# A recurrent time-mixing kernel on one core: three clearings move, and the last tile's store and logarithm are split differently

## The chip, the cores and the metric

One core of one Trainium2 chip. The metric is the device time of one execution in microseconds; lower is better. A core has five engines with a queue of instructions each: TensorE (PE in the profile; its weight loads are PEld), VectorE (DVE), ScalarE (ACT), GpSimd (POOL) and SyncE (SP). They run side by side and wait for one another through semaphores. DMAs are issued from SP, ACT or POOL and carried out by 16 DMA engines.

## What is computed

`w`, `u` have 256 channels; `k`, `v` and the output are 16 x 2048 x 256 in float32. For each batch and channel a recurrence runs over 2048 steps:

```python
ww = u + kk
qq = np.maximum(pp, ww)
e1 = np.exp(pp - qq); e2 = np.exp(ww - qq)
output[b, t, :] = (e1 * aa + e2 * vv) / (e1 * bb + e2 + 1e-08)
ww = pp - w + kk
qq = np.maximum(ww, kk)
e1 = np.exp(ww - qq); e2 = np.exp(kk - qq)
aa = e1 * aa + e2 * vv
bb = e1 * bb + e2
pp = qq
```

## The kernel before, in words

**Tiles.** 2048 steps are 16 stages (`NST`) of 128 steps. A stage has four tiles, each of four batches, so there are 64 tiles `n` (`NP`). A tile of `k` or `v` is 128 partitions x 4 x 256, 512 KB. Each stage's 128 steps are two halves of 64; within a half the recurrence is written as matrix products, and a small state passes from half to half.

**Per tile.** PE writes the rows of decay and bonus into PSUM (`rows`, L201: 64x64 pieces from `CO` and from the rows' tile `WU`, made of `w` and `u`) and adds the sums of `k` (`logs`, L207). ACT takes the exponential into `EZR` (L210). DVE or POOL casts `v` to bfloat16 (`cast_v`, L214), and DVE multiplies (`times_v`, L219). PE sums per half into `TOT` (`sums`, L245). Ten tiles later PE forms denominator and numerator (`apply`, L322, with the matrices `Id`, `IdN`, `S`, `SN`), ACT inverts the denominator as Exp(-Ln(x)) (L330 and L338, 128x1024 each), DVE multiplies (L350) and the result is stored in three pieces: 256 KB by SP (L363) and two of 128 KB (`piece`, L356), both by SP, or one by SP and one by POOL for the last tiles (`shared`). The very last tile, 63, is inverted and multiplied in two halves (`parts`).

**Per stage** a chain of small instructions turns the sums into the next state: `copy_sums`, `turn`, `state_logs` (ACT, L262), `state_frames` and on (DVE, on the small tiles `U`, `G`, `TB`), `state_spread` into `CB`, then four PE matmuls (`turn_back`, L302, with `Id`). Some elements of `U`, `G`, `TB` and `CB` are never written by that chain and must be cleared once beforehand.

**What sets the order.** Every part is a *step* with a due time (`place`). A loop at the end of the function takes, again and again, the step with the earliest due time whose predecessors are done and whose buffer is free, and writes its instructions into the engines' queues. The queues are in order. Every engine writes before this loop what stands ahead of it in the function: the start.

**The start, in the order of each queue.** DVE: clears `WUf`, the 128x256 tile that will hold `w` and `u` in a few of its rows (L124), then `M1`, `I1`, `Z`, `COf`, `Sel`, `low`; builds `NLE`, `NLZ`, `CO`, `OH` with POOL's selects and iotas between; clears the state's tiles (L231 to L236, nine memsets); then, as the first step of the loop (due time -9.17, `mats`), scales four matrices (L182); then the first rounding of `k` (`round_k`, L194), the rows' tile (`make_rows`, L175 and L176), the second rounding. POOL: the load of `u` into `WUf`, selects, iotas, selects, the loads of tiles 3 and on. ACT: the load of `w` into `WUf`, then the table of functions. SP: three loads of `k` and three of `v`. PE: 26 matmuls on zeros (`Z`, L149), which only keep it running, then 12 more and the first rows.

**The end.** The last tile's exponentials, products and stores, then a line of the launcher (L480): each engine drains, SP waits for every DMA, and the engines meet in a handshake.

Of the kernel before, what the change touches and what calls it, by code (L numbers as in the profile page):

```python
# [7 lines left out]
F32 = mybir.dt.float32  # L8
# [3 lines left out]
ACT = mybir.ActivationFunctionType  # L12
# [3 lines left out]
def kernel(  # L16
# [9 lines left out]
    K = tc.keep_in_program_order  # L26
    PE, DVE, SC, POOL, SP = nc.tensor, nc.vector, nc.scalar, nc.gpsimd, nc.sync
# [5 lines left out]
    D = 2 * Dm  # L33
    NP = 4 * NST
# [10 lines left out]
    RS = 2.0 ** -20  # L45
    CAP = 54.0
    BIG = 1e30
# [24 lines left out]
    rpool = ctx.enter_context(tc.tile_pool(name="rpool", bufs=NRD))  # L72
# [14 lines left out]
    def matrix(name, dt):  # L87
        return consts.tile([128, 128], dt, tag=name, name=name)
# [10 lines left out]
    def how(n):  # L99
        return "D" if n < BYSP else FIRST[n] if n < len(FIRST) else PLAN[n % len(PLAN)]  # L100
# [4 lines left out]
    def load_k(n):  # L105
        if how(n) != "C":
            KR[n] = raw(opool, "ot") if n < BYSP else raw(kppool, "kf")
            K((SP if n < BYSP else POOL).dma_start(out=KR[n], in_=rows_of(k, n)))  # L108
        else:
            KR[n] = kpool.tile([128, 4, Dm], F32R, tag="kr", name="kr")  # L110
            K(POOL.dma_start(out=KR[n], in_=rows_of(k, n)))
# [6 lines left out]
    WUf = rpool.tile([128, 2, D], F32, tag="rd", name="WUf")[:, 0, 0:Dm]  # L118
# [2 lines left out]
    def row_wu(queue, x, g):  # L121
        K(queue.dma_start(out=WUf[g::32, :], in_=bass.AP(tensor=x.tensor, offset=x.offset, ap=[[0, 4], list(x.ap[0])])))

    K(DVE.memset(WUf, 0.0))  # L124
    load_k(0)
    row_wu(POOL, u, 1)
    row_wu(SC, w, 0)
# [50 lines left out]
    mats = {name: matrix(name, BF16) for name in ("Id", "IdN", "S", "SN")}  # L178
# [11 lines left out]
    X = [psx.tile([128, 2, D], F32, tag=f"X{a}", name=f"X{a}") for a in range(2)]  # L190
# [31 lines left out]
    AS, D1, L1, A0, FR, BC, A2 = range(7)  # L222
    U_of = [consts.tile([128, 7, 32, 3], F32, tag=f"U{j}", name=f"U{j}") for j in range(2)]
    G_of = [consts.tile([128, 3, 32, 3], F32, tag=f"G{j}", name=f"G{j}") for j in range(2)]
    TB_of = [consts.tile([128, 2, 32, 3], F32, tag=f"TB{j}", name=f"TB{j}") for j in range(2)]
    CB_of = [consts.tile([128, 4, 128], BF16, tag=f"CB{j}", name=f"CB{j}") for j in range(2)]
    AB = consts.tile([128, 2, 32, 3], F32, tag="AB", name="AB")
    st = {}

    for j in range(2):  # L230
        K(DVE.memset(CB_of[j].bitcast(F32), 0.0))  # L231
        K(DVE.memset(U_of[j][:, FR, :, 0:1], -BIG))
        K(DVE.memset(G_of[j][:, :, :, 0:1], 0.0))
    K(DVE.memset(U_of[0][:, D1, :, 0:1], -100.0))
    K(DVE.memset(U_of[0][:, L1, :, 0:1], 0.0))
    K(DVE.memset(TB_of[0][:, :, :, 0:1], 0.0))  # L236

    def sums(n):
        c, p = divmod(n, 4)
# [70 lines left out]
    RD, NUM, OT = {}, {}, {}  # L310
# [14 lines left out]
    def den(n, a):  # L325
        apply(X[a], n, ("S", "Id"), 1)

    def log_den(n, a):
        rd = rpool.tile([128, 2, D], F32, tag="rd", name="rd")
        K(SC.activation(rd, X[a], ACT.Ln, scale=RS))  # L330
        RD[n] = rd

    def parts(n):
        return (slice(0, 1), slice(1, 2)) if n == NP - 1 else (slice(0, 2),)

    def inverse(n):
        for i in parts(n):
            K(SC.activation(RD[n][:, i], RD[n][:, i], ACT.Exp, scale=-1.0))  # L338

    def by_x(n):  # L340
        return n >= NP - XT and n % 2 == 1
# [11 lines left out]
    def piece(n, h, queue):  # L353
        c, p = divmod(n, 4)
        t0 = c * TC + HS * (1 - h)
        K(queue.dma_start(out=out[4 * p + 2:4 * p + 4, t0:t0 + HS, :].rearrange("n t d -> t n d"), in_=OT[n][HS * h:HS * h + HS, 2:4, :]))  # L356

    def shared(n):
        return n >= BYPOOL or BYQ[n % len(BYQ)] == "P" and n >= BYF
# [5 lines left out]
            piece(n, h, SP)  # L365

    def store_rest(n):
        piece(n, 1, POOL)


    ops, free = {}, {"K": NK, "KP": NKP, "V": NV, "N": 1, "RD": NRD, "OT": NOT, "VB": NVB}
# [1 line left out]
    def step(name, place, fn, args=(), after=(), take=None, give=(), mode=0):  # L373
        key = name if isinstance(name, str) else " ".join(map(str, name))
        ops[name] = dict(place=AT.get(key, place), fn=fn, args=args, after=list(after), take=take, give=give, mode=mode)

    for n in range(NP):
        c, j = divmod(n, 4)
        early = n < BYSP
        vb = "OT" if n < VOT else "V"  # L380
        put = lambda key: n + P[key][j]
        lead = SOON * max(0.0, 1 - n / UNTIL)
        lag = LAG - sum(n < x for x in LAGS)
        m = n + lag - lead
        tail = n >= NP - LAG
        place = lambda key: m + (P["TAIL"][key] + (n - NP + LAG) * P["TAIL"]["step"] if tail else P["OUT"][key][int(n + lag + 2) % 4])
        kb = "OT" if early else "KP" if how(n) != "C" else "K"
        if n:
            step(("LK", n), n + P["LK"], load_k, (n,), [("LK", n - 1)], kb)
        else:  # L390
            free["OT"] -= 1
        step(("LV", n), n + P["LV"], load_v, (n,), [("LV", n - 1)] + ([("LK", n)] if n else []), vb)
        if how(n) != "C":
            step(("RK", n), put("RK"), round_k, (n,), [("LK", n), ("RK", n - 1)], "K", [kb])
        for q in range(2):
            step(("R", q, n), n + P["R"][q], rows, (n, q), ["wu", ("R", 1 - q, n - 1 + q)], "X", mode=3)
            step(("L", q, n), n + P["L"][q], logs, (n, q), [("R", q, n), ("LK", n), ("RK", n), ("L", 1 - q, n - 1 + q)], None,
                 ["K"] if q else [], 1)
            step(("X", q, n), n + P["X"][q], exps, (n, q), [("L", q, n), ("NUM", n - RING), ("S", n - RING)], None, ["X"])
        step(("CV", n), put("CV"), cast_v, (n,), [("LV", n), ("CV", n - 1)], "VB", [vb])  # L400
        step(("TV", n), put("TV"), times_v, (n,), [("X", 1, n), ("CV", n), ("TV", n - 1)], None, ["VB"])
        step(("S", n), put("S"), sums, (n,), [("TV", n), ("S", n - 1)] + ([("CS", c - 1)] if j == 0 else []), mode=2)
        if j == 3:
            s = P["STATE"][0 if c == 0 else 2 if c == NST - 1 else 1]
            for i, (name, fn, *after) in enumerate((
                    ("CS", copy_sums, ("S", n)), ("TU", turn, ("CS", c), ("CH", c - 1)), ("SL", state_logs, ("TU", c)),
                    ("FR", state_frames, ("SL", c), ("SN", c - 1)), ("OF", state_offsets, ("FR", c)),
                    ("SW", state_weights, ("OF", c)), ("CH", state_chain, ("SW", c), ("KP", c - 1)),
                    ("SS", state_spread, ("CH", c)), ("TK", turn_back, ("SS", c), "mats"), ("BK", copy_back, ("TK", c)),
                    ("SN", state_next, ("OF", c)), ("KP", state_keep, ("CH", c)))):  # L410
                if not (name in ("SN", "KP") and c + 1 == NST):
                    step((name, c), n + s[i] - lead * SHARE, fn, (c,), after, mode=1)
        step(("DEN", n), place("DEN"), den, (n,), [("BK", c), ("DEN", n - 1), "mats"], "X", mode=3)
        step(("LN", n), place("LN"), log_den, (n,), [("DEN", n), ("INV", n - 1)], "RD", ["X"])
        step(("INV", n), place("INV"), inverse, (n,), [("LN", n)])
        step(("NUM", n), place("NUM"), num, (n,), [("BK", c), ("TV", n), ("NUM", n - 1), "mats"], "X" if by_x(n) else "N", mode=3)
        step(("MUL", n), place("MUL"), mult, (n,), [("NUM", n), ("INV", n), ("MUL", n - 1)], "OT", ["X" if by_x(n) else "N", "RD"])
        step(("ST", n), place("ST"), store, (n,), [("MUL", n), ("ST", n - 1)], None, [] if shared(n) else ["OT"])
        if shared(n):
            step(("SQ", n), place("SQ"), store_rest, (n,), [("ST", n)], None, ["OT"])  # L420
    step("mats", P["mats"], make_matrices)
    step("wu", P["wu"], make_rows)

    quiet = False
# [60 lines left out]
```

## Time and profile before

| | us |
|---|---|
| runs of the kernel before | 290.93, 292.04, 292.12 (median 292.04) |
| profiled execution, whole | 291.05 |
| its span, first to last instruction | 289.3 |

| engine | busy us | share of the span | instructions |
|---|---|---|---|
| PE | 272.0 | 94% | 3263 |
| PEld | 139.5 | 48% | 3263 |
| DVE | 246.1 | 85% | 423 |
| ACT | 258.1 | 89% | 290 |
| POOL | 176.9 | 61% | 219 |

The DMAs moved 101.21 MB at a mean of 350 GB/s; in the first 30 us, when there are only loads, 348 to 350 GB/s from 8 us on.

How to read it: a line of the profile names engine, source line, operation, output<-input and shape. Times are from the span's start. "Idle before" is the time for which the engine stood still ahead of an instruction, and what ended that. The granted clock of TensorE was 0.988 of full speed over the span. A `q` behind an engine's name (SPq, POOLq) marks its sequencer: DMA issues, semaphores, drains.

### The profile page before, as it was taken

To read this page: it belongs to the slowest core of one execution; us is meant where nothing else is said; L and a number is where in the kernel's file an instruction comes from. 1 tells how busy PE (TensorE), PEld (TensorE's weight loads), DVE (VectorE), ACT (ScalarE), POOL (GpSimd) and SP (SyncE) were. 2 spreads that over 40 slices of the span, in tenths; PEclk is the share of its full clock that TensorE was granted. 3 is DMA by queue.
4 is the path that set the end of the run, shared out by engine and by line. 5 is a ranking of instruction groups with operands and counts; after the bars stand their busy time and mean duration, and the time that the engine had idled before them with its cause. 6 is when DMAs were issued, how large, how long until landed. Compare 5 with 4: busy or idle time off the path is not lost.

```text
span 289.3 us, 8057 instructions
## 1 busy us (share of the span) xinstructions
PE 272.0 (94%) x3263; PEld 139.5 (48%) x3263; DVE 246.1 (85%) x423; ACT 258.1 (89%) x290; POOL 176.9 (61%) x219
## 2 busy tenths in 40 slices
PE   7899999999999999999999999999999999997750
PEld 6445744444545455444545454554545455444330
DVE  6666889989898989899897979899898989797860
ACT  1587399999999999999999999999999999997890
POOL 7267367675767686675757686775757674422230
PEclk9999999999999999999999999999999999999995
DMA  7999999999999999999999999999999999896895
GB/s 229 351 347 347 348 343 337 382 328 392 386 393 380 371 387 377 393 383 392 391 381 382 385 385 388 392 365 397 391 391 382 389 363 390 294 247 180 221 265 147
DMA packets 58574, 101.21 MB, mean 350 GB/s; under 512 B 5152, under 2 KB 43560, under 8 KB 58536
## 3 DMA queue, kind: packets, MB, share of 16 engines
q0 software_dynamic: 21248, 65.55, 65.2%
q1 hardware_dynamic: 37280, 35.14, 36.3%
q8 instruction: 25, 0.41, 0.6%
q14 instruction: 13, 0.11, 0.1%
q10 hardware_dynamic: 8, 0.00, 0.0%
HBM read 67.12 MB, written 33.55 MB: 348 GB/s over the span
## 4 chain that ended last, share of the span: by engine, by line
PE 83%; DVE 4%; ACT 4%; issue 3%; POOL 1%; DMA 1%; POOLq 0%; SPq 0%; DVEq 0%
PE X L207 21%; PE X L322 15%; PE num L322 13%; PE X L201 12%; PE TURN L149 12%; PE TOT L245 7%; ACT EZR L210 2%; PE TOT L258 2%; DVE ot L350 1%; PE TURN L302 1%; POOL out_dram L356 1%; DMA out_dram<-ot 1%; ACT rd L330 1%; DVE EZR L219 1%; ACT rd L338 1%
## 5 line engine op out<-in xcount | busy, mean ns | idle before, releaser
L210 ACT ACTIVATE EZR<-X 128x1024 bf16<-128x1024 f32 x128 | 126.8, 1013 | 14.2 <-PE X L207 14.1
L214 POOL CAST vb<-vr 128x1024 bf16<-128x1024 f32 x54 | 56.3, 1042 | 69.7 <-DVE EZR L219 68.1
L219 DVE TENSOR_TENSOR EZR<-EZR,vb 128x2048 bf16<-128x2048 bf16 x64 | 77.8, 1218 | 0.4 <-ACT EZR L210 0.2
L350 DVE TENSOR_TENSOR ot<-num,rd 128x1024 f32<-128x1024 f32 x60 | 73.2, 1220 | 4.6 <-ACT rd L338 3.2
L338 ACT ACTIVATE rd<-rd 128x1024 f32<-128x1024 f32 (+1 forms) x65 | 67.9, 1046 | 2.0
L330 ACT ACTIVATE rd<-X 128x1024 f32<-128x1024 f32 x64 | 65.6, 1025 | 2.5 <-PE X L322 0.9
L149 PE MATMUL TURN<-Z 128*128 128x192 bf16 x319 | 55.7, 261 | 1.6 <-DVE Z L133 1.6
L201 PE MATMUL X<-WU,CO 64*64 64x512 bf16 x512 | 51.9, 390 | 1.1 <-DVE WU L176 0.9
L149 PEld LDWEIGHTS <-Z 128*128 128x128 bf16 x319 | 28.9, 101 | 48.9 <-issue 47.1
L115 POOL DMA_DIRECT2D vr<-in_v_dram x61 | 46.0, 753 | 6.5 <-DVE vb L214 6.5
L207 PE MATMUL X<-kr,NLE 128*128 128x512 f32 x128 | 45.6, 438 | 0.0
L207 PE MATMUL X<-kr,NLZ 128*128 128x512 f32 x128 | 45.5, 437 | 0.0
L108 POOL DMA_DIRECT2D kf<-in_k_dram x53 | 40.2, 758 | 0.0
L194 DVE CAST kr<-kf 128x1024 fp32r<-128x1024 f32 x39 | 30.6, 813 | 4.4 <-DMA kf<-in_k_dram 4.2
L201 PEld LDWEIGHTS <-CO 64*64 64x64 bf16 x512 | 15.7, 105 | 31.4 <-issue 26.4
L322 PE MATMUL X<-EZR,S 64*64 64x512 bf16 x256 | 26.2, 394 | 1.7 <-ACT rd L330 1.0
L322 PE MATMUL X<-cb,Id 64*64 64x512 bf16 x256 | 25.8, 376 | 0.0
L322 PE MATMUL X<-EZR,Id 64*64 64x512 bf16 x256 | 25.8, 376 | 0.0
L322 PE MATMUL num<-EZR,SN 64*64 64x512 bf16 x240 | 24.3, 386 | 1.1 <-DVE ot L350 1.1
L322 PE MATMUL num<-cb,IdN 64*64 64x512 bf16 x240 | 24.0, 376 | 0.0
L322 PE MATMUL num<-EZR,IdN 64*64 64x512 bf16 x240 | 23.9, 376 | 0.0
L245 PE MATMUL TOT<-EZR,OH 128*32 128x256 bf16 x512 | 23.4, 277 | 0.5 <-DVE EZR L219 0.5
(69 smaller groups left out, 270.0 us busy)
## 6 DMA issues: line engine op xcount, KB each, us to landing
vr<-in_v_dram POOLq DMA_DIRECT2D x61, 512.0 KB, 7.9
kf<-in_k_dram POOLq DMA_DIRECT2D x53, 512.0 KB, 8.8
out_dram<-ot SPq DMA_DIRECT2D x64, 256.0 KB, 10.2
out_dram<-ot SPq DMA_DIRECT2D x116, 128.0 KB, 10.1
kr<-in_k_dram POOLq DMA_DIRECT2D x8, 512.0 KB, 8.2
ot<-in_k_dram SPq DMA_DIRECT2D x3, 512.0 KB, 5.0
ot<-in_v_dram SPq DMA_DIRECT2D x3, 512.0 KB, 8.3
out_dram<-ot POOLq DMA_DIRECT2D x12, 128.0 KB, 3.3
```

The source lines that it names most:

```text
L115: K((SP if n < BYSP else POOL).dma_start(out=vr, in_=rows_of(v, n)))
L149: K(PE.matmul(TURN[:, 0:192], Z[:, 0:128], Z, start=first, stop=True, skip_group_check=True))
L201: K(PE.matmul(X[a][o:o + HS, i, :].rearrange("p (n d) -> p n d", n=2), CO[r:r + HS, q, :], WU[r:r + HS, :].unsqueeze(1).broadcast_to([HS, ...
L207: K(PE.matmul(X[a][:, i, :], (NLE, NLZ)[q], km[:, i, :], start=False, stop=True, skip_group_check=True))
L210: K(SC.activation(ez(n)[:, q, 1], X[a], ACT.Exp))
L214: K((DVE if n < EARLY else POOL).tensor_copy(vb, VR.pop(n)))
L219: K(DVE.tensor_mul(ez(n)[:, :, 0], ez(n)[:, :, 1], vb.unsqueeze(1).broadcast_to([128, 2, 2, D])))
L245: K(PE.matmul(t[32 * j:32 * j + 32, 0:256], OH[:, s:s + 32], ez(n)[:, 0, 1 - q, i, 256 * x:256 * x + 256], start=p == 0 and x == 0, stop=p ...
L322: K(PE.matmul(out_tile[o:o + HS, i, :], left, right, start=s == 0, stop=s == 2, tile_position=(r, o), skip_group_check=True))
L330: K(SC.activation(rd, X[a], ACT.Ln, scale=RS))
L338: K(SC.activation(RD[n][:, i], RD[n][:, i], ACT.Exp, scale=-1.0))
L350: K(DVE.tensor_mul(o.rearrange("p (i n) d -> p i (n d)", i=2)[:, i], NUM[n][:, i], RD[n][:, i]))
```

## The change

Four edits. (1) `WUf` is cleared by POOL instead of DVE, ahead of POOL's load of `u`. (2) The nine clearings of the state's tiles become a step, `zero`, with due time 1.01, and the first `state_logs` waits for it. (3) The scaling of the four matrices, `mats`, gets the due time 1.0 instead of -9.17. Both steps then stand on DVE behind the second cast of `v` and ahead of the third. (4) For tile 63 the logarithm is taken by halves, each half's Exp right behind it, and the last 128 KB piece of the store is issued by ACT instead of POOL.

```diff
-    K(DVE.memset(WUf, 0.0))
+    K(POOL.memset(WUf, 0.0))
...
-    for j in range(2):
-        K(DVE.memset(CB_of[j].bitcast(F32), 0.0))
-        K(DVE.memset(U_of[j][:, FR, :, 0:1], -BIG))
-        K(DVE.memset(G_of[j][:, :, :, 0:1], 0.0))
-    K(DVE.memset(U_of[0][:, D1, :, 0:1], -100.0))
-    K(DVE.memset(U_of[0][:, L1, :, 0:1], 0.0))
-    K(DVE.memset(TB_of[0][:, :, :, 0:1], 0.0))
+    def start_states():
+        for j in range(2):
+            K(DVE.memset(CB_of[j].bitcast(F32), 0.0))
+            K(DVE.memset(U_of[j][:, FR, :, 0:1], -BIG))
+            K(DVE.memset(G_of[j][:, :, :, 0:1], 0.0))
+        K(DVE.memset(U_of[0][:, D1, :, 0:1], -100.0))
+        K(DVE.memset(U_of[0][:, L1, :, 0:1], 0.0))
+        K(DVE.memset(TB_of[0][:, :, :, 0:1], 0.0))
...
-    def log_den(n, a):
-        rd = rpool.tile([128, 2, D], F32, tag="rd", name="rd")
-        K(SC.activation(rd, X[a], ACT.Ln, scale=RS))
-        RD[n] = rd
-
     def parts(n):
         return (slice(0, 1), slice(1, 2)) if n == NP - 1 else (slice(0, 2),)
 
+    def log_den(n, a):
+        RD[n] = rpool.tile([128, 2, D], F32, tag="rd", name="rd")
+        for i in parts(n):
+            K(SC.activation(RD[n][:, i], X[a][:, i], ACT.Ln, scale=RS))
+            if i.stop == 1:
+                invert(n, i)
+
+    def invert(n, i):
+        K(SC.activation(RD[n][:, i], RD[n][:, i], ACT.Exp, scale=-1.0))
+
     def inverse(n):
-        for i in parts(n):
-            K(SC.activation(RD[n][:, i], RD[n][:, i], ACT.Exp, scale=-1.0))
+        invert(n, parts(n)[-1])
...
     def store_rest(n):
-        piece(n, 1, POOL)
+        piece(n, 1, POOL if n < NP - 1 else SC)
...
-                    ("CS", copy_sums, ("S", n)), ("TU", turn, ("CS", c), ("CH", c - 1)), ("SL", state_logs, ("TU", c)),
+                    ("CS", copy_sums, ("S", n)), ("TU", turn, ("CS", c), ("CH", c - 1)), ("SL", state_logs, ("TU", c), "zero"),
...
-    step("mats", P["mats"], make_matrices)
+    step("mats", 1.0, make_matrices)
+    step("zero", 1.01, start_states)
```

## The prediction

> **What bounds the kernel now.** I read the page first: PE is busy 94% of the span, ACT 89%, and the chain that ended last is 83% PE. From 30 to 200 us PE has under 0.3 us idle, and its order of instructions doesn't change, so the change can act in two places: how early PE's first tile starts, and what stands after its last one. So I then read the chain in order of time over the first 30 us (start, length, what):
>
> ```profile
> 4.59 0.27 DVE CB L231
> ...
> 5.60 0.50 DVE IdN L182
> 6.10 0.07 DVE S L182
> 6.17 0.13 DVE SN L182
> 6.30 0.60 DVE kr L194
> 6.90 0.41 DVE WU L175
> 7.33 0.49 DVE WU L176
> 7.87 0.41 PE X L201 x4
> ```
>
> The reader is to see that VectorE alone leads to PE's first real work at 7.87, and that 4.59 to 6.23 is clearing and matrices that this tile doesn't use. That is 1.64 us, the most that the front can give. The next question is what else the rows' tile WU waits for. The row u, asked for by tile:
>
> ```profile
> L122 POOL DMA_DIRECT2D WUf<-in_u_dram x1: 747/747/747, 1.5 to 1.5; - x1
> ...
> DMA to landing us min/median/max: 5.0/5.0/5.0
> ```
>
> Issued at 1.51, it lands at 6.56 by the trace; w lands at 5.53, the first k (issued 0.81) at 4.85. For the end I read the timeline of ACT, DVE, SP and POOL, one fence for each, and then the instructions of the closing line:
>
> ```profile
> 279.56 1.00 ACT L330 ACTIVATE rd<-X 128x1024 f32<-128x1024 f32 x1
> 280.60 1.15 ACT L338 ACTIVATE rd<-rd 128x512 f32<-128x512 f32 x2
> ```
> ```profile
> 281.26 1.29 DVE L350 TENSOR_TENSOR ot<-X,rd 128x512 f32<-128x512 f32 x2 [0.35 <-ACT rd L338]
> ```
> ```profile
> 282.06 0.54 SPq L363 DMA_DIRECT2D out_dram<-ot  x1
> 282.70 0.60 SPq L356 DMA_DIRECT2D out_dram<-ot  x1
> ```
> ```profile
> L480 SPq DRAIN  x2: 7/7/7, 287.2 to 287.2; - x2
> ...
> L480 POOLq DRAIN  x1: 5381/5381/5381, 282.8 to 282.8; - x1
> L480 POOLq EVENT_SEMAPHORE  x1: 17/17/17, 288.2 to 288.2; - x1
> ```
>
> Of the last tile's three stores, GpSimd's is issued at 282.84. SP's land by 286.79 and GpSimd's at 286.56; SP has seen every landing by 287.24. But GpSimd's closing drain runs from 282.82 for 5.38 us, to 288.20, and the final handshake (288.2 to 289.3) starts only then. **The end waits 0.96 us for GpSimd's drain alone.**
>
> **Front, part by part.**
> - WUf's clearing on GpSimd. No GpSimd memset of this size is in the trace. Lower bound 0.10 (the 128x1 constants), upper 0.60 (two 128x128 selects at 0.30); by the nearest row, the 128x1024 cast at 1.04 for four times the elements, 0.26, and with some start I take 0.33. GpSimd is released at 0.70, so it starts at about 0.85 and ends at 1.18, where VectorE's ended at 1.21. GpSimd's own DMA then starts after 0.05 (between two of its iotas) to 0.30 (its last store after VectorE): 1.23 to 1.48, I take 1.38 against 1.51. So u is issued 0.13 earlier and, the queue ahead of it being the same, lands at 6.43; by the bounds (memset 0.10 or 0.60) 6.05 to 6.8. w is never last. VectorE's first memsets move up by 0.25, and so do Z and PE's 38 filler matmuls, which end at 6.75.
> - The block behind VectorE's first work. It leaves 4.59 to 6.23. The rounding of k then starts when k lands, 4.87, and ends at 5.55; WU now waits for u, 6.43, and starts at 6.47 instead of 6.83. **Front gain 0.36 us** (0 to 0.75): of the 1.64 removed, 1.28 turns into a wait for u. PE's rows start at 7.51; the fillers (6.75) don't hold them.
> - Where the block goes. The instruction order puts it behind the second v cast, at about 13.85. Queued behind it: the third v cast (next start 0.61 later), then the product of tile 1 (L219, 1.21 us), for which PE's sums wait. That product ended at 16.18; now 13.85 + 1.64 + 0.61 + 1.21 = 17.31. PE's waiting matmul came at 18.04 and comes at 17.68: 0.37 us of cover is left, cost nothing. From 19.97 VectorE was idle for 3.25 us before `ts`; that takes up the rest. The first users, the state's logarithm at 27.13 and the matmuls at 33.03, are far off.
> - Does the gain last? Early loads land one each 1.5 us from 4.85 to 45 us at 348 GB/s whatever is asked, so they don't move with PE. The closest is k of tile 6: landed at 22.76, used at 23.49, 0.73 us of cover. A gain of 0.36 passes, one over 0.7 would be cut. Beyond tile 10 the cover is 4 us or more, and in the tail the waits are on engines, so it reaches the end.
>
> **Tail.** Half activations here start 0.54 apart and last 0.62. Before: Ln 279.56 to 280.57, Exp halves end at 281.23 and 281.75. After: Ln, Exp, Ln, Exp, each Exp waiting for its own Ln: ends at 280.81 and 281.96. The first product can start at 280.9 instead of 281.26, the last at 282.0 instead of 281.87 (+0.12). So the half tile's 256 KB store leaves 0.35 earlier and the two last pieces 0.12 later, at 282.82, with less ahead of them. I take their last landing as unchanged, 286.8 (286.3 to 287.3, by the 3.2 to 4.1 us that such pieces took). GpSimd's last DMA is now that of the tile before, issued at 281.21, landed at 284.68. Its drain ended 1.65 after its landing and 5.36 after its issue; by the one 286.3, by the other 286.6. Both are ahead of SP's 287.24, so SP ends it: **tail gain 0.96** (0.5 to 1.4).
>
> The Trainium skill, "DMA: Bandwidth & Descriptors", section "Issuing engines are not separate DMA queues", says that spreading DMAs over engines saves only the sequencer's issue time. By it the move to ScalarE would be worth the 0.14 us between SP's and GpSimd's issue. The landings agree with it (286.56 and 286.79); the drain's row is what it leaves out.
>
> **Sum.** The profiled execution took 291.05 (span 289.33 and 1.72 around it). 291.05 - 0.36 - 0.96 = 289.7, and the span 288.0. The runs shown are 290.93, 292.04 and 292.12; the mean of these and the profiled one is 291.54, and the median is 1.0 above the profiled one. From 291.54 less 1.32 I forecast **290.2**, a gain of 0.45%. About 0.5%, 1.46 us, is what a measurement of this kernel can tell from no change, so the forecast is just inside it.
>
> **Rivals.**
> - *The front gives nothing.* GpSimd's memset and start take 0.37 more, u lands at 6.8 and WU starts where it did. For it: the upper bound of the memset; u's wait replaces the whole block. 291.54 - 0.96 = 290.6.
> - *GpSimd's drain doesn't follow its last store* (a fixed cost at the close), or ScalarE's piece lands 1 us later: the only row of ScalarE's queue, w, needed 4.3 us under load. Only the front and 0.14 of issue are left: 291.0. Against it: ACT's and DVE's drains end 0.05 after their last work.
> - *Slower: the moved block stretches and stalls PE's sums.* At 13.85 it stands beside GpSimd's issues of k and v (13.49 to 15.35), where before it stood beside two others; there IdN took 0.50 and S 0.44 where Id took 0.18 and SN 0.21, and a k issue 1.13 instead of 0.75. If each of its 13 instructions grew by 0.3 us, it would be 5.5 us long, and PE would lose 3.9 - 0.37 = 3.5: 291.54 - 1.32 + 3.5 = 293.7. It decides for slower from a length of 1.64 + 0.37 + 1.32 = 3.3 us on. Against it: the measured 1.64 includes that stretch already.
> - The Trainium skill, "SBUF — State Buffer", section "SBUF: two separate sides", has such a rule: VectorE in a 2-port mode and GpSimd's descriptor writing lock each other out. The longer k issue above would fit it; no row shows the block in its new place.
> - *The change doesn't do what it says:* the instruction order shows each move as described, and PE's and SP's orders unchanged.
>
> **How the numbers follow.** Forecast 0.64, front nothing 0.14, drain stays 0.12, slower by the block 0.06, others 0.04. Faster by over 0.5%: nearly half of the forecast's own spread (0.5 to 2.1 us) lies beyond 1.46 (0.31), and 0.07 comes from the others: 0.38. Slower by over 0.5%: 0.07, the block and a little. Within: 0.55. The range: 291.54 less 2.1, and the runs' own half microsecond, gives 288.9; up, the drain's case 291.0 plus the same spread, 291.7.
>
> **What would show it.** Right: WU starts at 6.4 to 6.5 with a DMA wait ahead of it, PE's rows at 7.5, no new PE wait at L246, GpSimd's drain ending by 286.6 and SP's last. Wrong: u landing at 6.8 or later; a wait of PE for VectorE near 17.7; a GpSimd drain that still ends over 0.5 us after SP's; ScalarE's piece landing after 287.3.

## The result, and the profile after

The changed kernel took 290.18 us (median of 20 runs, 289.38 to 291.55), the kernel before beside it 291.68 (20 runs, 290.93 to 292.29). The ratio is 0.9948, 95% interval [0.9939, 0.9957]: 1.50 us faster, where 1.32 was forecast. The total came out close to the forecast here; three further comparisons below give 1.29, 0.87 and 0.73 us, all less than it. Two of the steps that led to the sum did not hold, and a loss in the middle that the prediction did not see decides how much arrives.

The profiled execution after is the longest of the 20 (291.55, span 289.8). So a second one, "the change again" (289.91, span 288.2), is read beside it; below it is called a_again.

*The front.* The chain in order of time after the change (start, length, what):

```profile
0.80 0.32 POOL WUf L124
1.12 0.29 issue
1.42 5.69 DMA WUf<-in_u_dram
...
7.13 0.30 DVE WU L175
...
7.46 0.49 DVE WU L176
...
7.99 0.41 PE X L201 x4
```

The clearing took 0.32 us and `u` was issued at 1.42, as worked out (0.33; 1.38). The chain now leads through the DMA of `u`, not through VectorE's matrices. But `u` landed at 7.11 here, later than before (6.56). The change again (a_again), same view:

```profile
1.37 5.70 PE TURN L149 x38
7.07 0.34 PE X L201 x4
```

Here `u` landed at 5.99 and the rows' tile started at 6.01, so neither `u` nor VectorE is last: PE's 38 filler matmuls are, and they end at 7.07.

*The tail after.* ACT, then DVE, each by its timeline:

```profile
280.36 0.58 ACT L335 ACTIVATE rd<-X 128x512 f32<-128x512 f32 x1
280.97 0.63 ACT L340 ACTIVATE rd<-rd 128x512 f32<-128x512 f32 x1
281.50 0.58 ACT L335 ACTIVATE rd<-X 128x512 f32<-128x512 f32 x1
282.11 0.63 ACT L340 ACTIVATE rd<-rd 128x512 f32<-128x512 f32 x1
283.50 0.72 ACTq L361 DMA_DIRECT2D out_dram<-ot  x1
```
```profile
281.63 0.69 DVE L355 TENSOR_TENSOR ot<-X,rd 128x512 f32<-128x512 f32 x1
282.77 0.69 DVE L355 TENSOR_TENSOR ot<-X,rd 128x512 f32<-128x512 f32 x1 [0.45 <-ACT rd L340]
```

And the launcher's closing line (durations in ns; first and last start in us):

```profile
L486 POOLq DRAIN  x3: 46/227/5626, 282.0 to 289.6; - x3
L486 SPq DRAIN  x3: 7/7/7, 288.6 to 288.9; - x3
```

GpSimd's long drain runs from 281.98 for 5.63 us, to 287.61, and SP's last wait ends at 288.6: SP ends the kernel now, 1.0 us behind GpSimd. Before, GpSimd ended 0.96 behind SP.

From the start of the last logarithm to the span's end: 9.77 us before, 9.47 here, 8.60 in the change again. All of PE's last tile came 0.79 later than before in the one and 0.04 later in the other. So 291.05 + 0.79 - 0.30 gives the 291.55 of the one, and 291.05 + 0.04 - 1.17 the 289.91 of the other. The front's gain, 0.86 us at PE's rows in the change again (7.01 against 7.87), is no longer there at the last tile. Where it went is what the experiments are for.

### The profile page after: what moved, and what is told of

It reads as the page before. It is cut to its first block, busy times and chain, and to the rows that moved or that the text cites. A ratio compares the mean times of both kernels' runs of the same rounds, so it can differ in the third digit from the quotient of the medians.

```text
span 289.8 us, 8058 instructions
## 1 busy us (share of the span) xinstructions
PE 272.7 (94%) x3263; PEld 139.8 (48%) x3263; DVE 245.7 (85%) x422; ACT 258.7 (89%) x291; POOL 176.7 (61%) x219
## 4 chain that ended last, share of the span: by engine, by line
PE 80%; ACT 8%; DVE 4%; DMA 3%; issue 2%; POOL 0%; SPq 0%; DVEq 0%; POOLq 0%
PE X L207 20%; PE X L323 15%; PE num L323 12%; PE X L201 12%; PE TURN L149 12%; PE TOT L246 7%; ACT rd L335 3%; ACT EZR L210 3%; DVE ot L355 2%; ACT rd L340 2%; DMA WUf<-in_u_dram 2%; PE TOT L259 2%; PE TURN L303 1%; DMA out_dram<-ot 1%; DVE EZR L219 1%
## 5 line engine op out<-in xcount | busy, mean ns | idle before, releaser
L335 ACT ACTIVATE rd<-X 128x1024 f32<-128x1024 f32 (+1 forms) x65 | 65.8, 1012 | 2.8 <-PE X L323 1.0
L149 PE MATMUL TURN<-Z 128*128 128x192 bf16 x319 | 56.4, 265 | 1.4 <-DVE Z L133 1.4
L149 PEld LDWEIGHTS <-Z 128*128 128x128 bf16 x319 | 29.5, 103 | 48.7 <-issue 47.1
L207 PE MATMUL X<-kr,NLE 128*128 128x512 f32 x128 | 45.6, 438 | 0.0
L207 PE MATMUL X<-kr,NLZ 128*128 128x512 f32 x128 | 45.5, 437 | 0.0
L194 DVE CAST kr<-kf 128x1024 fp32r<-128x1024 f32 x39 | 31.1, 825 | 6.4 <-DMA kf<-in_k_dram 6.3
```

Source lines behind the costliest of these rows:

```text
L149: K(PE.matmul(TURN[:, 0:192], Z[:, 0:128], Z, start=first, stop=True, skip_group_check=True))
L207: K(PE.matmul(X[a][:, i, :], (NLE, NLZ)[q], km[:, i, :], start=False, stop=True, skip_group_check=True))
L335: K(SC.activation(RD[n][:, i], X[a][:, i], ACT.Ln, scale=RS))
```

## The experiments

Each ratio is to the kernel before, run beside it on the same chip.

### The parts alone

*front_only*: edits 1 to 3, with tile 63 as before.

> Only the front's edits: WUf cleared by GpSimd, the state's clearing and the matrices behind the second v cast; the last tile as before. Theory: 0.36 us faster, ratio 0.9988 (0.9975 to 1.000), and GpSimd's drain still ends the span, about 1 us after SP's last wait. Rival (the front gives nothing since u's landing takes the place of the block): ratio 1.000. Rival (the front gives all of it and the drain hides nothing): 0.995.

291.25 us, 1.0009 [0.9988, 1.0029]; no gain that can be told. (Its profile is of the longest of its 12 runs, 293.60.) *store_only* is the kernel before and

```diff
-        piece(n, 1, POOL)
+        piece(n, 1, POOL if n < NP - 1 else SC)
```

> Only the last 128 KB piece by ScalarE instead of GpSimd. Theory: GpSimd's drain follows its last store's landing by 1.6 us, so it now ends at about 286.3 from the span's start, SP's waits end the span at 287.2, gain 0.96, ratio 0.9967. Rival (only issue time is saved): gain 0.14, ratio 0.9995, and the drain ends as late as before. Rival (ScalarE's piece lands later than GpSimd's did, as in the profile shown: 4.7 us after its issue): gain 0.3 to 0.5, ratio 0.9985.

290.57 us, 0.9971 [0.9958, 0.9985]: the gain is here. Its closing line:

```profile
L480 POOLq DRAIN  x3: 51/93/5137, 281.5 to 288.4; - x3
L480 SPq DRAIN  x3: 7/7/7, 287.5 to 287.8; - x3
```

GpSimd's drain ends at 281.52 + 5.14 = 286.66, which is 1.60 after GpSimd's last DMA landed (285.06). In the other 13 profiles it ended 1.60 to 1.64 us behind that landing (before: 286.56 and 288.20), whenever it had started. It follows the last store that GpSimd issued. *halves_only* is the kernel before and

```diff
...
-        K(SC.activation(rd, X[a], ACT.Ln, scale=RS))
...
+            K(SC.activation(RD[n][:, i], X[a][:, i], ACT.Ln, scale=RS))
+            if i.stop == 1:
+                invert(n, i)
...
```

> Only the last tile's logarithm by halves. Theory: the first half's store leaves 0.35 earlier and the last two pieces 0.12 later, and GpSimd's drain still ends the span: 0.0 to 0.12 slower, ratio 1.0000 to 1.0005. Rival (with less ahead of them the last pieces land earlier): 0.2 to 0.3 faster, ratio 0.999.

291.80 us, 1.0007 [0.9992, 1.0022]: nothing by itself. *a_again* is the whole change:

> The changed kernel once more, for a second profile: the first one shown is the slowest of its 20 executions (291.55 against a median of 290.18) and had one DMA engine late from the second load on (u landed at 7.11 us) and two losses of about 0.4 us near 125 and 150 us. Theory (gain 0.36 in front and 0.96 at the end): a ratio of 0.9948 again; in a typical execution u lands at 6.3 to 6.6, WU starts at 6.4 to 6.6, PE's first rows at 7.4 to 7.6, GpSimd's drain ends 1.6 us after its last landing and before SP's last wait. Rival (front nothing, all of it at the end): the same ratio, but WU at 6.8 or later and PE's rows at 7.85 or later here too.

290.12 us, 0.9955 [0.9941, 0.9969].

### Does the front's gain reach the end?

I followed the start of PE's logarithm matmul (L207) tile by tile against the kernel before. The change again was 0.87 ahead at tiles 0 to 3, 0.45 at tiles 6 to 11, 0.28 at tile 13, held that to tile 26, and was 0.28 *behind* at tile 27 and 0.06 at tile 29. The first theory (A) was that loads at the DMA engines' limit eat any lead. *tail_only* has edit 4 alone.

> Before with both edits of the tail and none of the front. Theory A (the front's lead does not reach the end: the steady loads use the DMA engines fully, and a tile that runs ahead waits for its k until the lead is gone, by tile 27 in the trace of the whole change): as fast as the whole change, ratio 0.9945 to 0.9960 to before and within 0.1% of a_third. Theory B (in typical executions a front gain of about 0.36 us does reach the end): 0.996 to 0.997 to before, 0.10 to 0.15% slower than a_third. Both: last landing about 7.0 us after the last logarithm starts, where the ScalarE store alone had 7.27, because the first half of the last product leaves 0.35 us earlier and SP, no longer GpSimd, ends the kernel.

290.82 us, 0.9977 [0.9967, 0.9988].

> The whole change, unaltered, beside tail_only on one chip. Ratio 0.9945 to 0.9960 to before, span about 288.2, PE's first rows at 7.0 and the lead over before gone by about tile 27. If A holds tail_only is within 0.1% of this; if B holds this is 0.10 to 0.15% faster.

290.49 us, 0.9964 [0.9951, 0.9977]. The difference of 0.13% is that of theory B, with intervals that overlap. The traces speak plainer, and against A: in a_third the lead was 0.42 at tile 13 and 0.44 at tile 30; in tail_only, with no lead to lose, PE fell back too, by 0.35 at tile 31 and again at tile 39. The loss comes in steps of one size, always at tiles 4m + 3 ("step" means such a loss from here on). *tail_light* is tail_only once more, one execution:

> The tail's edits only, unaltered, one look in the same order of runs as its light pair: span 288.2 to 288.8, PE's start at 7.87 and no steps or one of 0.36 us in its distance to before in the middle.

290.81 us, PE's rows at 7.87, one step (tile 47), as expected.

What a step is shows in VectorE's and GpSimd's timelines. Before, at tile 27, no step:

```profile
103.51 1.04 POOL L214 CAST vb<-vr 128x1024 bf16<-128x1024 f32 x1 [0.53 <-DVE EZR L219]
103.92 1.17 DVE L194 CAST kr<-kf 128x1024 fp32r<-128x1024 f32 x1
104.49 1.50 POOL L194 CAST kr<-kf 128x1024 fp32r<-128x1024 f32 x1
105.12 1.23 DVE L350 TENSOR_TENSOR ot<-num,rd 128x1024 f32<-128x1024 f32 x1
```

The change again, same place:

```profile
103.22 1.04 POOL L214 CAST vb<-vr 128x1024 bf16<-128x1024 f32 x1 [0.53 <-DVE EZR L219]
104.20 1.04 POOL L194 CAST kr<-kf 128x1024 fp32r<-128x1024 f32 x1
104.22 1.56 DVE L194 CAST kr<-kf 128x1024 fp32r<-128x1024 f32 x1 [0.74 <-DMA kf<-in_k_dram]
...
105.71 1.21 DVE L355 TENSOR_TENSOR ot<-num,rd 128x1024 f32<-128x1024 f32 x1
...
106.97 0.41 PE L323 MATMUL num<-EZR,SN 64*64 64x512 bf16 x4 [0.38 <-DVE ot L355]
```

The reader is to see the order of the two L194, each engine's rounding of a `k` of its own. Before, VectorE's rounding started ahead of GpSimd's; it ended 0.54 after GpSimd's cast of `v` (105.09 against 104.55), and GpSimd's rounding stretched to 1.50, which nobody waits for. In the second, VectorE's `k` landed 0.02 us too late. GpSimd's rounding went first in 1.04, and VectorE's ended 0.54 behind *it* (105.78 against 105.24). VectorE's product, next in its queue, came late, and PE waited. Which of the two starts first is a race that the landing of `k` decides, and they exclude each other: alone VectorE's rounding takes 0.68 and GpSimd's 1.04.

The Trainium skill, "SBUF — State Buffer", section "SBUF: two separate sides", calls the port pair of VectorE and GpSimd an exclusive lock that the first to start holds for the whole instruction. The trace agrees: in the 11 profiles with the usual order, every VectorE rounding that started during GpSimd's ended 0.54 to 0.59 us after it.

The next table has what each profile shows. A shift is that of PE's logarithm matmul of the tile against before (minus is earlier); "second" counts VectorE's roundings from tile 13 on that came second. Each row is one execution; those of after, front_only, tail_only and tail_late are the longest of their runs.

| profile | `u` landed | PE rows | shift, tile 13 | second | shift, tile 63 |
|---|---|---|---|---|---|
| before | 6.56 | 7.87 | 0 | 0 | 0 |
| after | 7.11 | 8.00 | +0.13 | 2 | +0.79 |
| a_again | 5.99 | 7.01 | -0.28 | 1 | +0.04 |
| a_third | 5.79 | 6.68 | -0.42 | 3 | +0.59 |
| a_fourth | 6.14 | 7.03 | +0.05 | 1 | +0.30 |
| front_only | 6.14 | 7.03 | -0.05 | 4 | +2.30 |
| store_only | 6.72 | 7.87 | 0 | 1 | +0.34 |
| halves_only | 6.65 | 7.87 | 0 | 1 | +0.34 |
| tail_only | 6.66 | 7.88 | 0 | 2 | +0.65 |
| tail_light | 6.69 | 7.87 | 0 | 1 | +0.37 |
| all_light | 5.86 | 7.49 | -0.33 | 0 | -0.41 |
| all_late | 5.63 | 7.36 | +0.77 | 0 | +0.74 |
| tail_late | 6.79 | 7.87 | +0.55 | 0 | +0.53 |
| all_late15 | 5.85 | 6.75 | -0.37 | 0 | -0.37 |

Except in front_only (near 123 us VectorE waited 2.31 us there for its `k`, and PE 1.33 us for VectorE's product), the shift at tile 63 is that at tile 13 and 0.35 us for each rounding that came second, to 0.1 us.

### Taking the race away

*all_late* is the change and GpSimd's rounding of every fourth `k` placed later, behind its next two load issues; no other queue's order changes. *tail_late* is tail_only with the same edit.

```diff
-    P = {"LK": -4.45, "LV": -3.2, "RK": [-2.85, -1.165, -3.305, -1.485], "L": [-12.055, -8.285],
+    P = {"LK": -4.45, "LV": -3.2, "RK": [-2.85, -1.165, -3.305, -1.15], "L": [-12.055, -8.285],
```

*all_light* is the change with less for the DMA engines to carry; it leaves the first 256 KB store of tiles 4 to 47 out of its output:

```diff
-        K(SP.dma_start(out=out[4 * p:4 * p + 2, c * TC:(c + 1) * TC, :].rearrange("n t d -> t n d"), in_=OT[n][:, 0:2, :]))
+        if not 4 <= n < 48:
+            K(SP.dma_start(out=out[4 * p:4 * p + 2, c * TC:(c + 1) * TC, :].rearrange("n t d -> t n d"), in_=OT[n][:, 0:2, :]))
```

*a_fourth* is the change beside them.

> The whole change again, beside the next three on one chip. 0.9945 to 0.9965 to before; in its trace zero to three steps of 0.35 us at tiles 19, 23, 27 and so on, each where VectorE's rounding of k starts after GpSimd's has begun.

290.75 us, 0.9965 [0.9950, 0.9981]; one step.

> The whole change, and GpSimd's rounding of every fourth k placed behind its next k and v issues, so 1.5 us later; no other engine's order changes. Theory C (the steps of 0.35 us come from the order in which VectorE's and GpSimd's roundings start: whichever is second ends 0.55 us behind the first): GpSimd's now starts at least 1.2 us behind VectorE's even when k is late, so no step is left, a late k costs only what it is late beyond 0.34 us, PE's lead of 0.3 to 0.45 at tile 13 is there at tile 63, and the time is 0.3 to 0.8 us below a_fourth (two steps on average in the traces with the front's edits). Theory D (the steps come from the k that lands late by itself, and the two roundings only stretch each other): the steps stay, same time as a_fourth within 0.1%. A third outcome: GpSimd's later rounding holds up PE's logarithms of its own tile, wanted 1.7 us after it ended before, and the kernel is slower.

290.62 us, 0.9966 [0.9952, 0.9980]. No step from tile 13 to 63, as theory C has it; but PE lost 1.3 us at tiles 11 and 12, the third outcome, and the time is that of a_fourth. From tile 13 on one `k` alone was late here, at tile 47, and it shows the mechanism. It was about as late as the one above (VectorE's rounding started 5.14 us after the one before it, there 5.16), and GpSimd was free 0.01 us before it; where its rounding would have stood, there is now a load issue:

```profile
186.13 1.02 POOL L108 DMA_DIRECT2D kf<-in_k_dram  x1
186.14 0.69 DVE L194 CAST kr<-kf 128x1024 fp32r<-128x1024 f32 x1 [0.72 <-DMA kf<-in_k_dram]
186.77 1.23 DVE L355 TENSOR_TENSOR ot<-num,rd 128x1024 f32<-128x1024 f32 x1
...
188.34 0.41 PE L323 MATMUL num<-EZR,SN 64*64 64x512 bf16 x4
```

VectorE's rounding takes 0.69 instead of 1.56, and PE waits for nothing. So this late landing alone cost nothing; the order of the two roundings makes the step. The loss begins with the later rounding at the one tile that has little time, 11:

```profile
41.95 1.42 POOL L194 CAST kr<-kf 128x1024 fp32r<-128x1024 f32 x1
...
43.43 0.72 PE L207 MATMUL X<-kr,NLE 128*128 128x512 f32 x2 [0.51 <-POOL kr L194]
```

> The same placing of GpSimd's rounding in the kernel with the tail's edits alone. Theory C: no step, PE's start at 7.87 and tile 63 at 253.36 or a few hundredths from it, 0.3 to 0.5 us below tail_only's 0.9977 of before, that is 0.9960 to 0.9967; and 0.3 to 0.45 us above all_late, which is what the front's edits are then worth at the end. If the lead is lost in another way, tail_late and all_late are within 0.1%.

290.87 us, 0.9977 [0.9964, 0.9991]. No step; 0.55 lost at tile 12 and held to tile 63. The trace shows the wait:

```profile
41.74 1.51 DVE L267 TENSOR_TENSOR U<-U 128x64 f32<-128x64 f32 x1
42.10 1.05 POOL L194 CAST kr<-kf 128x1024 fp32r<-128x1024 f32 x1
...
45.56 0.40 PE L245 MATMUL TOT<-EZR,OH 128*32 128x256 bf16 x6 [0.16 <-DVE EZR L219]
```

GpSimd's later rounding held a small product of the state's chain, 1.51 us long instead of 0.21 (in all_late 1.05). `times_v`, behind it in VectorE's queue, started at 44.29 instead of 43.15, and PE waited for it. So the later rounding avoids one meeting and makes another, at this tile.

> The whole change without the first 256 KB store of tiles 4 to 47, which this kernel leaves out of its output: the engines' work is the same, the DMA engines carry about a sixth less in the middle. If the late k come from the DMA engines being full, VectorE's rounding is ahead of GpSimd's at every tile behind 20, there is no step, the lead of 0.3 to 0.45 us holds to tile 63 (252.9 to 253.1) and the time is 0.9932 to 0.9950 to before. If the steps come without full DMA engines, they stay.

289.68 us, 0.9935 [0.9918, 0.9953]: no step, and the lead holds, -0.33 at tile 13 and -0.41 at tile 63. The sums of 50 to 240 us, all_light, then a_third (length; busy us and instructions of PE, PEld, DVE, ACT and POOL; granted clock; DMA share, where packets' times are added up and can pass 1; GB/s):

```profile
50.00:240.00 190.00, 189.67 (x2322) 93.73 (x2318) 178.33 (x281) 187.06 (x212) 133.20 (x152) 1.00 0.98 331
```
```profile
50.00:240.00 190.00, 188.57 (x2306) 92.59 (x2298) 175.87 (x280) 186.79 (x212) 131.73 (x151) 1.00 1.05 385
```

With 331 instead of 385 GB/s moved, VectorE's rounding never waited for its `k`; a_third had eight such waits, 4.3 us. So by these traces it takes both: DMA engines so full that `k` lands just in time, and the order of the two roundings.

*all_late15* places GpSimd's rounding later from tile 15 on only:

```diff
-            step(("RK", n), put("RK"), round_k,
+            step(("RK", n), put("RK") + (0.335 if j == 3 and n > 11 else 0), round_k,
```

> The whole change with GpSimd's rounding behind its next k and v issues from tile 15 on, and where it was for tile 11. In the two kernels that had it later at tile 11 too, PE lost 0.6 to 1.3 us once at tiles 11 and 12 and nothing from tile 13 to 63. Theory C with that cost as one of tile 11 alone: PE's lead at tile 13 (0 to 0.45 us, by whether an early k cut it) is there at tile 63 to 0.05, no rounding of VectorE starts behind GpSimd's after tile 20, and the time is 0.9930 to 0.9955 to before, 0.4 to 0.9 us below what the whole change had in its last two runs (0.9964 and 0.9965). If the loss at tile 12 was the later rounding's cost at any tile, PE loses 0.5 us again at tile 15 or 16 and the time is that of all_late (0.9966).

289.56 us, 0.9931 [0.9915, 0.9948]: 1.95 us faster than before and the fastest of the study. The lead of 0.37 at tile 13 is 0.37 at tile 63. VectorE waited for its `k` five times (1.9 us in all) at no cost. Only one of the five, at tile 47, was so late that GpSimd's rounding would have been ahead in its old place (VectorE's started at 185.05, GpSimd was free at 185.03), so this and the one in all_late are the meetings that test the new order. At tile 27, with `k` in time:

```profile
103.32 1.40 DVE L194 CAST kr<-kf 128x1024 fp32r<-128x1024 f32 x1
104.12 0.91 POOL L108 DMA_DIRECT2D kf<-in_k_dram  x1
104.74 1.23 DVE L355 TENSOR_TENSOR ot<-num,rd 128x1024 f32<-128x1024 f32 x1
...
105.77 1.05 POOL L194 CAST kr<-kf 128x1024 fp32r<-128x1024 f32 x1
```

It did not run on one chip with the change; the change's four ratios are 0.9948, 0.9955, 0.9964 and 0.9965.

## Why the prediction was right, and where its steps failed

**Tail, 0.96 (0.5 to 1.4): right in mechanism and about in size.** GpSimd's drain follows its last store, and SP ends the kernel once that store is another's. store_only measured 0.84 us (291.41 - 290.57), tail_only 0.54 (291.36 - 290.82), both below 0.96. From last logarithm to span's end the four profiles of the change took 9.47, 8.60, 8.54 and 9.14, mean 8.94, against 9.77: 0.83. The spread is that of the last landing, "unchanged, 286.8" in the prediction, 7.2 us behind the last logarithm. It was 7.83, 6.95, 6.88 and 7.50 behind it. The rival that the drain doesn't follow the last store fell.

**The logarithm by halves** was given nothing of its own in the sum, and has none that could be told: alone 1.0007, and tail_only against store_only 0.9977 and 0.9971. The first product did start earlier, 1.27 us after the last logarithm began instead of 1.70, and the last ended 0.12 later.

**The Trainium skill's rule on issuing engines ("DMA: Bandwidth & Descriptors", section "Issuing engines are not separate DMA queues").** By it the move to ScalarE was worth 0.14 us. It measured 0.84 in store_only. The landings of the last pieces do agree with it: ScalarE's came 0.17 to 0.28 us after SP's in the four profiles of the change, for issues at about the same time. The prediction's sign of a late ScalarE piece (after 287.3) did show in two of them, 288.19 and 287.35, but SP's piece was as late, so the rival that ScalarE's queue is slower fell. What the rule leaves out is the engine's own drain.

**Front, u issued at 1.38 and landing at 6.43.** The issue came at 1.42 and the clearing took 0.32: right. The landing was 5.79 to 6.14 in a_again, a_third and a_fourth and 7.11 in the profile after. Against 6.56 before, an issue 0.09 us earlier was worth 0.77 in one execution and -0.55 in another. Of all eight profiles with the front's edits, seven have the landing at 5.63 to 6.14; the six without have it at 6.56 to 6.79. So the gain is mostly larger than the issue's 0.09, and why is not known.

**"PE's rows start at 7.51; the fillers (6.75) don't hold them": wrong.** That took the fillers' length from one profile, 1.65 to 7.00. They start 0.16 us apart and later 0.083 apart, and the moment of that change differs from execution to execution (4.2 to 7.1 us, and not before the last of the 38 in all_light). Started at 1.37, the 38 ended at 7.07 in a_again and held the rows; where that moment came early (a_third, all_late15) the rows' tile was last and the rows started at 6.7.

**The block behind the second `v` cast: at no cost, as worked out.** The rival that it stretches fell. In a_again it took from 13.30 to 15.10 and behind it VectorE waited for the next `v`:

```profile
13.30 0.41 DVE L182 TENSOR_SCALAR Id<-I 128x128 bf16<-128x128 f32 x1
...
14.99 0.11 DVE L237 MEMSET TB<- 128x64 f32 x1
15.49 0.69 DVE L214 CAST vb<-ot 128x1024 bf16<-128x1024 f32 x1 [0.38 <-DMA ot<-in_v_dram]
```

In a_fourth PE did wait 0.59 us for VectorE at 18.05, near the 17.7 that the prediction gave as a sign of being wrong. But there too VectorE stood idle behind the block, 0.57 us until that `v` landed: the load was late, not the block.

**"A gain of 0.36 passes, one over 0.7 would be cut": right.** Of 0.87, 0.45 were left at tile 6 in a_again, and of 1.19, 0.50 in a_third, where PE waited 0.4 us for that tile's `k`. In a_fourth loads were later still and the whole 0.84 was gone at tile 4.

**"Beyond tile 10 the cover is 4 us or more ... so it reaches the end": the step that failed.** The cover was measured from the landing of `k` to PE's use of it. Between them stands VectorE's rounding, in order ahead of a product that PE wants at once, and in a race with GpSimd's rounding. There the profile of before had little to spare: VectorE waited for its `k` at seven tiles from 13 on (3.1 us in all), and its rounding started 0.57 us ahead of GpSimd's at tile 27 and 0.09 at tile 43. Each lost race costs about 0.35, and the profiles with the usual order lost none to four. A smaller part goes at tile 12 (0.46 to 0.28 in a_again): GpSimd's cast of a `v` and VectorE's rounding of a `k`, both waiting for their loads, started 0.3 to 0.4 us later than in before (39.71 against 39.40, 41.16 against 40.80), and VectorE's work behind them with them.

**So what arrives of the front?** The two pairs on one chip give 0.33 us (a_third against tail_only) and 0.25 (all_late against tail_late), each with overlapping intervals; front_only changed the time by -0.35 to +0.84 us. So the rival that the front gives nothing to the total is not excluded by the times of the change itself; its reason, that the rows' tile would start where it did (6.83), fell: it started at 6.01 in a_again. By the traces the lead at tile 13 was 0.4 to none, and 0.37 and 0.41 arrived only in all_late15 and all_light, where no race was lost. Races were lost 2.2 times on average in the five profiles with the front's edits and the usual order (all_light left out), and 1.0 times in the five without the edits; with so few it stays open whether the lead itself makes them more likely. That the total came out at 1.50 for 1.32 is in part luck: the four comparisons of the same change gave 1.50, 1.29, 0.87 and 0.73 us. And the profile of before, from which the terms were read, had lost no race, while the kernel's medians were 0.3 to 0.6 us above it (291.36 to 291.68 against 291.05).

## What to carry to other kernels

A load's cover is counted to the first instruction that touches it, and from there to whoever stands behind that instruction in its queue, not to the last user. Where VectorE and GpSimd both cast, look which is ahead at each meeting, and place the one that nobody waits for so late that the other can't come second; then look what it meets in its new place, which cost 0.6 and 1.3 us at tiles 11 and 12 here. At the end of a kernel, ask what each engine's drain waits for: a last small store from GpSimd cost 0.84 us (store_only) that no chain of landings shows.

## What the runs showed of the hardware

- GpSimd's closing drain ended 1.60 to 1.64 us after the landing of the last DMA that GpSimd had issued, and so can end after SP's wait for all of them.
- A VectorE rounding of 128x1024 (0.68 us alone) and a GpSimd cast of that size (1.04) don't overlap: whichever starts second is held until the first is done. VectorE's then ends 0.54 to 0.59 us later, and GpSimd's takes up to 1.57 (a_again).
- A VectorE product of 128x64 that met GpSimd's rounding was held too: 1.51 us in tail_late and 1.05 in all_late instead of 0.21, ending 0.1 us behind it.
- A GpSimd load issue that met a VectorE rounding under way or starting with it took 0.90 to 1.03 us instead of 0.75 (tile 11 and on). Where the issues were under way first, at tile 11 of tail_late and all_late, VectorE's rounding took 0.83 and 1.58.
- `u`, issued at 1.42 behind two loads of 512 KB, landed from 4.2 to 5.7 us later in the eight profiles with the front's edits.
